# Building the S5 tables of a two-layer hybrid trunk without GpSimd, dealt out per weight unit of the first feed-forward network

## The chip, the cores and the metric

The kernel runs on one NeuronCore of a Trainium2 chip. The metric is device time in microseconds (us) of one execution. The engines are named TensorE (PE in rows), VectorE (DVE), ScalarE (ACT), GpSimd (POOL) and SyncE (SP), whose queue issues nearly all transfers; PEld in rows is TensorE's weight load.

## The reference, cut to what matters

The model is two layers on a sequence of 512 tokens of width 1024. Each layer is feed-forward network (FFN), token mixer, FFN; the first layer's mixer is an S5 state-space layer, the second's a convolution module. So there are six sub-layers: ffn0, s5, ffn2, ffn3, conv, ffn5. The first two matter here:

```python
def swiglu(h, w1, w3, w2):                # w1, w3: 1024 x 2816, w2: 2816 x 1024
    return (jax.nn.silu(h @ w1) * (h @ w3)) @ w2

# s5_mixer, for each of 64 groups of 16 channels, 64 complex states:
    mag = jnp.exp(dt * ar)
    abar_re = mag * jnp.cos(dt * ai)
    abar_im = mag * jnp.sin(dt * ai)
    f_re = (nr * ar + abar_im * ai) / den
    f_im = (abar_im * ar - nr * ai) / den
    bb_re = f_re[..., None] * br - f_im[..., None] * bi
    bb_im = f_re[..., None] * bi + f_im[..., None] * br
```

The recurrence state(t) = abar * state(t-1) + bb * u(t), read out by c, is computed in blocks of steps. For that the kernel needs tables that depend on the parameters alone: powers of abar (turns), input tables from f and b, output products of c with powers of abar, and short kernels c * abar^k * bb laid out as a Toeplitz block.

## The kernel before, in words

**Matrix products.** Every weight is loaded by SP as a unit of 128x1024 (eight blocks of 128x128; line 84) and split in two halves, a high one cast by ScalarE (L95) and a low one that is the difference (L99), by VectorE or, while `lo_engine` says so, by GpSimd. `mm3` (L111 to L113) runs three matmuls of 512 columns a block: high by high, high by low, low by high. So a unit is 24 matmuls.

**The first FFN.** The up product takes 44 units, two for each of 22 output blocks m: one unit for w1, one for w3. m = 0 and 1 belong to the entry, the loop in `ffn` takes m = 2 to 21. The block before is evacuated by five operations in a fixed order: VectorE L399, ScalarE L400 (silu), VectorE L401, ScalarE L403, VectorE L404. The down product (`proj`) takes 22 units. `want(n)` splits units ahead of their use, one or two units ahead.

**The tables.** They are made while ffn0 runs, stored to `tab_d` in device memory, and read back by the S5 layer. `s5_params` is a chain of small VectorE operations (128x32). `s5_turn` first doubles a table H on VectorE (L638 to L640), then for each of eight tiles a table E in three steps of 128x64, 128x128 and 128x256 on GpSimd (L652 to L654). `s5_ops` makes, for each of eight tiles, output products with c (L735 to L737: four powers in 128x512, a fifth in 128x128; the imaginary half on GpSimd), products with b (L749 to L751, 128x128), copies on ScalarE (L755), kernels on TensorE (L698) and their Toeplitz layout on VectorE (L710 to L716). The tables b and c come with the zero blocks of a pair of groups in them, and the products run over those too. `s5_in` makes the input tables: each tile loads one block of b (L664) and four of f (L667, from `f_d`), runs six 128x512 operations on VectorE (L674 to L680) and stores (L681).

**What sets the order.** Each engine runs its instructions in the order in which the Python program emits them. The table builders are generators in queues named D, E, Q, K, T and P. `pump(q, n)` takes n steps from queue q. How many a block m gets is written by hand in `PACE_D`, `PACE_E`, `PACE_Q0` and `PACE_Q1`; the down product takes one step of P at every eighth matmul group; what is left is flushed behind the down product.

```python
            pump("D", PACE_D[m - 2])
            pump("E", PACE_E[m - 2])
            pump("Q", PACE_Q1[m - 2])
            lo_engine[0] = POOL if bg["D"] and not bg["E"] else DVE
```

Of the kernel before, what the change touches and what calls it, by code (L numbers as in the profile page):

```python
# [7 lines left out]
F32 = mybir.dt.float32  # L8
# [3 lines left out]
P = 128  # L12
# [24 lines left out]
def trunk(ctx: ExitStack, tc: tile.TileContext, h, plan):  # L37
# [103 lines left out]
    bg = {q: [] for q in "DEKTQP"}  # L141

    def pump(q, n=1):
        while n and bg[q]:
            if next(bg[q][0], StopIteration) is StopIteration:
                bg[q].pop(0)
            else:
                n -= 1

    def flush():  # L150
        while any(bg.values()):
            for q in "DEQKTP":
                pump(q)
# [84 lines left out]
    def proj(u0, nk, rhs, post, nl, pre, xn, bias=None, lead=None, carried=None, defer=True):  # L238
# [154 lines left out]
    def ffn(e, post, pre, defer=True):  # L393
# [15 lines left out]
        for m in range(2, NF):  # L409
            ready = len(bg["K"])  # L410
            pump("Q", PACE_Q0[m - 2])
            pa, pb = psum(), psum()
            for j, ps in enumerate((pa, pb)):
                want(u0 + 2 * m + j)
                for k in range(NK):
# [3 lines left out]
                    if j == 1 and k == 3 and ready:  # L419
                        pump("K")  # L420
# [31 lines left out]
    def s5_params(tb, F):  # L452
# [6 lines left out]
        ar, ai, ldt = (prm[:, 32 * i : 32 * i + 32] for i in range(3))  # L459
        free = [s[:, j, :] for s in scr for j in range(32)]  # L460
# [4 lines left out]
        def tt(a, b, op, o=None):  # L465
            o = new() if o is None else o
# [3 lines left out]
        def ts(a, c, op, c2=None, op2=None, o=None):  # L470
            o = new() if o is None else o
# [6 lines left out]
        def stt(a, c, b, op, op2, o=None):  # L478
            o = new() if o is None else o
# [33 lines left out]
        def sincos(v, c, s):  # L513
# [97 lines left out]
        def turned():  # L611
# [3 lines left out]
            bg["T"].append(store(pst))  # L615
            yield
# [10 lines left out]
    def s5_turn(tb):  # L627

        H = page(F32).rearrange("p r (q c) -> p r q c", c=16)
        w = page(F32).rearrange("p r (q c) -> p r q c", c=16)  # L630
        DVE.memset(H[:, 0, :, 0:1], 1.0)
        DVE.memset(H[:, 1, :, 0:1], 0.0)
        for j in range(4):
            n = 1 << j
            er, ei = (v[:, j, :].unsqueeze(2).to_broadcast([P, 32, n]) for v in (tb["er"], tb["ei"]))
            re, im = H[:, 0, :, :n], H[:, 1, :, :n]
            for d, (p, q, op) in enumerate((((re, er), (im, ei), ALU.subtract), ((re, ei), (im, er), ALU.add))):
                DVE.tensor_tensor(w[:, 0, :, :n], p[0], p[1], op=ALU.mult)  # L638
                DVE.tensor_tensor(w[:, 1, :, :n], q[0], q[1], op=ALU.mult)
                DVE.tensor_tensor(H[:, d, :, n : 2 * n], w[:, 0, :, :n], w[:, 1, :, :n], op=op)  # L640
            yield
        for i in range(8):
            E = page(F32).rearrange("p r (q c) -> p r q c", q=4)
            w = page(F32).rearrange("p r (q c) -> p r q c", q=4)
            s = slice(4 * i, 4 * i + 4)
            ACT.copy(E[:, :, :, 0:16], H[:, :, s, :])  # L646
            for j in range(4, 7):
                n = 1 << j
                er, ei = (v[:, j, s].unsqueeze(2).to_broadcast([P, 4, n]) for v in (tb["er"], tb["ei"]))
                re, im = E[:, 0, :, :n], E[:, 1, :, :n]  # L650
                for d, (p, q, op) in enumerate((((re, er), (im, ei), ALU.subtract), ((re, ei), (im, er), ALU.add))):
# [6 lines left out]
    def s5_in():  # L658
# [11 lines left out]
        nxt = load(0)  # L670
        for i in range(8):
            (bt, fb), nxt = nxt, load(i + 1) if i < 7 else None
# [3 lines left out]
            DVE.tensor_tensor(fb[:, 1, :], fb[:, 0, :], bt[:, 1, :], op=M)  # L676
            yield
# [3 lines left out]
            nc.sync.dma_start(out=tab_d[i, :, 0:1024], in_=flat(fb))  # L681
            yield

    def s5_ops(tb, F):
# [742 lines left out]
```

## Time and profile before

| | |
|---|---|
| median of 3 runs | 1966.86 us (1965.58 to 1968.68) |
| the profiled execution | 1966.77 us, its span 1965.0 us |
| TensorE busy | 1878.3 us (96% of the span) |
| VectorE busy | 1144.3 us (58%) |
| ScalarE busy | 608.8 us (31%) |
| GpSimd busy | 227.0 us (12%), nearly all in the first 600 us |

TensorE is busy nearly everywhere, so the time is the sum of its matmuls, plus the places where it waits, plus the places where its clock is low. The share of busy time does not tell the last two apart: a matmul at half clock counts as busy, too. One has to look at the granted clock and at the waits, stretch by stretch.

### The profile page before, as it was taken

To read this page: it belongs to the slowest core of one execution; us is meant where nothing else is said; L and a number is where in the kernel's file an instruction comes from. 1 tells how busy PE (TensorE), PEld (TensorE's weight loads), DVE (VectorE), ACT (ScalarE), POOL (GpSimd) and SP (SyncE) were. 2 spreads that over 40 slices of the span, in tenths; PEclk is the share of its full clock that TensorE was granted. 3 is DMA by queue.
4 is the path that set the end of the run, shared out by engine and by line. 5 is a ranking of instruction groups with operands and counts; after the bars stand their busy time and mean duration, and the time that the engine had idled before them with its cause. 6 is when DMAs were issued, how large, how long until landed. Compare 5 with 4: busy or idle time off the path is not lost.

```text
span 1965.0 us, 23884 instructions
## 1 busy us (share of the span) xinstructions
PE 1878.3 (96%) x9374; PEld 1591.5 (81%) x9374; DVE 1144.3 (58%) x1796; ACT 608.8 (31%) x856; POOL 227.0 (12%) x269
## 2 busy tenths in 40 slices
PE   9978799999679999999999999999999999999997
PEld 7766588888568988888898888888888898888886
DVE  6888875758965853433267343323996785443324
ACT  5222232233214542322135222212512554232211
POOL 2437523012740000000000000000000000000000
PEclk9989899999889999999999999999999999999998
DMA  4234436945822233222223232232374023323231
GB/s 156 97 106 135 127 129 184 286 161 212 293 75 86 76 130 106 89 94 90 92 76 127 98 105 88 66 117 97 127 254 161 29 90 129 107 86 95 79 106 43
DMA packets 100129, 236.11 MB, mean 120 GB/s; under 512 B 26032, under 2 KB 41904, under 8 KB 100016
## 3 DMA queue, kind: packets, MB, share of 16 engines
q1 hardware_dynamic: 98720, 233.51, 36.2%
q8 instruction: 73, 1.20, 0.3%
q10 hardware_dynamic: 1296, 1.07, 0.2%
q14 instruction: 40, 0.33, 0.0%
HBM read 210.82 MB, written 23.72 MB: 119 GB/s over the span
## 4 chain that ended last, share of the span: by engine, by line
PE 79%; DVE 16%; issue 2%; ACT 1%; DMA 1%; POOL 1%; POOLq 0%; DVEq 0%; SPq 0%; ACTq 0%
PE ps L113 25%; PE ps L112 25%; PE ps L111 25%; PE ps L1141 2%; DVE pg L99 2%; DVE pg L467 1%; DVE pg L834 1%; PE ps L1108 1%; DVE x L341 1%; DVE tmp L337 1%; DVE pg L737 1%; DVE pg L844 1%; DVE pg L735 1%; DVE pg L736 1%; DVE tmp L401 1%
## 5 line engine op out<-in xcount | busy, mean ns | idle before, releaser
L113 PE MATMUL ps<-pg,pg 128*128 128x512 f32 (+1 forms) x2808 | 1033.6, 368 | 24.9 <-DVE pg L99 22.5
L111 PE MATMUL ps<-pg,pg 128*128 128x512 f32 (+1 forms) x2808 | 1039.3, 370 | 9.1 <-ACT pg L1275 4.7
L112 PE MATMUL ps<-pg,pg 128*128 128x512 f32 (+1 forms) x2808 | 1033.9, 368 | 4.9 <-DVE pg L173 3.4
L113 PEld LDWEIGHTS ps<-pg,pg 128*128 128x128 f32 x2808 | 533.3, 190 | 115.8 <-DVE pg L99 25.9
L111 PEld LDWEIGHTS ps<-pg,pg 128*128 128x128 f32 x2808 | 533.4, 190 | 97.6 <-ACT pg L1275 5.1
L112 PEld LDWEIGHTS ps<-pg,pg 128*128 128x128 f32 x2808 | 533.0, 190 | 97.4 <-DVE pg L173 8.2
L99 DVE TENSOR_TENSOR pg<-raw,pg 128x1024 fp32r<-128x1024 f32 x295 | 358.7, 1253 | 97.6 <-ACT pg L95 61.0
L95 ACT CAST pg<-raw 128x1024 fp32r<-128x1024 f32 x310 | 310.7, 1047 | 127.5 <-DMA raw<-w 28.2
L401 DVE TENSOR_TENSOR tmp<-ps,tmp 128x512 f32<-128x512 f32 x88 | 60.9, 692 | 247.3 <-PE ps L113 218.3
L263 DVE TENSOR_TENSOR acc<-acc,tmp 128x512 f32<-128x512 f32 (+1 forms) x54 | 33.0, 611 | 265.3 <-ACT tmp L258 265.2
L400 ACT ACTIVATE tmp<-tmp 128x512 f32<-128x512 f32 x88 | 55.6, 632 | 318.9 <-DVE tmp L399 318.9
L403 ACT CAST pg<-tmp 128x512 fp32r<-128x512 f32 x88 | 54.6, 621 | 249.9 <-DVE tmp L401 249.1
L258 ACT ACTIVATE tmp<-ps 128x512 f32<-128x512 f32 (+1 forms) x45 | 24.3, 539 | 300.8 <-PE ps L113 300.4
L404 DVE TENSOR_TENSOR pg<-tmp,pg 128x512 fp32r<-128x512 f32 x88 | 61.3, 696 | 61.1 <-ACT pg L403 61.1
L399 DVE TENSOR_TENSOR tmp<-ps,y 128x512 f32<-128x512 f32 x88 | 60.5, 688 | 27.3 <-PE ps L113 27.1
L160 ACT ACTIVATE pg<-x,gsc 128x256 fp32r<-128x256 f32 x80 | 40.8, 510 | 67.9 <-DVE x L341 67.9
L1055 DVE SCALAR_TENSOR_TENSOR pg<-pg,vec,pg 128x512 f32<-128x512 f32 x79 | 53.0, 741 | 0.0
L173 DVE SCALAR_TENSOR_TENSOR pg<-x,gsc,pg 128x256 fp32r<-128x256 f32 (+1 forms) x88 | 48.5, 553 | 2.3 <-ACT pg L201 1.8
L652 POOL TENSOR_TENSOR pg<-pg,pg 128x64 f32<-128x64 f32 (+2 forms) x48 | 27.6, 575 | 162.9 <-ACT pg L646 160.0
L341 DVE SCALAR_TENSOR_TENSOR x<-tmp,gsc,x 128x256 f32<-128x256 f32 x96 | 45.8, 478 | 0.0
L1141 PEld LDWEIGHTS ps<-pg,pg 128*128 128x128 f32 x360 | 41.0, 192 | 0.4
L1141 PE MATMUL ps<-pg,pg 128*128 128x128 f32 x360 | 41.0, 275 | 0.0
(163 smaller groups left out, 1059.2 us busy)
## 6 DMA issues: line engine op xcount, KB each, us to landing
raw<-w SPq DMA_DIRECT2D x262, 512.0 KB, 4.0
pg<-tab_d SPq DMA_DIRECT2D x24, 512.0 KB, 6.3
pg<-toep SPq DMA_DIRECT2D x20, 512.0 KB, 5.8
tab_d<-pg SPq DMA_DIRECT2D x16, 512.0 KB, 3.3
raw<-cv_w_in SPq DMA_DIRECT2D x16, 512.0 KB, 4.6
pg<-s5b SPq DMA_DIRECT2D x8, 512.0 KB, 8.8
pg<-f_d SPq DMA_DIRECT2D x32, 128.0 KB, 8.0
raw<-s_w_in SPq DMA_DIRECT2D x8, 512.0 KB, 4.2
```

Source lines behind the costliest of these rows:

```text
L95: ACT.copy(hv, r)
L99: lo_engine[0].tensor_tensor(lv, r, hv.bitcast(F32), op=ALU.subtract)
L111: PE.matmul(out, lhsT=hi[:, s, :], rhs=xh, start=start, stop=False)
L112: PE.matmul(out, lhsT=hi[:, s, :], rhs=xl, start=False, stop=False)
L113: PE.matmul(out, lhsT=lo[:, s, :], rhs=xh, start=False, stop=stop)
L341: DVE.scalar_tensor_tensor(x[:, k, cs], t[:, cs], gsc[:, post + k : post + k + 1], x[:, k, cs], op0=ALU.mult, op1=ALU.add)
L399: DVE.tensor_tensor(a, pa, e["y"], op=ALU.mult)
L400: ACT.activation(a, a, AF.Silu)
L401: DVE.tensor_tensor(a, pb, a, op=ALU.mult)
L403: ACT.copy(t[:, 0, :], a)
L404: DVE.tensor_tensor(t[:, 1, :], a, t[:, 0, :].bitcast(F32), op=ALU.subtract)
L1141: PE.matmul(ps[:, q * P : q * P + P], lhsT=op[ND * q + d], rhs=z[:, q, 8 - d : 8 - d + P], start=d == 0, stop=d == ND - 1,)
```

## The change

GpSimd no longer takes part in the tables, except that it clears buffers. The low halves of all weights, the E steps and all products go to VectorE. The products run without the zero blocks: c and b come packed (the host lays out `s5b` with 256 + 128 columns where it had 640), VectorE works on 128x320 (five powers at once) and 128x64, and ScalarE copies the results to their places between zeros. The Toeplitz layout is one VectorE addition in PSUM and four ScalarE copies. The hand-written paces are replaced by `tick(q, budget)`: each piece of work adds an estimate of its VectorE time to `cost`, and a tick hands out work until its credit is spent. In the up product there is a tick at every unit (two for each m), in the down product one at every unit. Tiles 0 and 1 of `s5_ops` stay in the up product, tiles 2 to 7 and then `s5_in` go to the down product. The loads of the parameters and of the identity move to the start of the program.

The diff, cut to its core (`...` marks what is left out):

```diff
+PREP_UP, PREP_DOWN = 2.8, 3.4
+S5_FIRST = 2
...
+    def tick(q, budget):
+        for stage in "TK":
+            now, bg[stage] = bg[stage], []
+            for g in now:
+                if next(g, StopIteration) is not StopIteration:
+                    bg[stage].append(g)
+        credit[0] += budget
+        while bg[q] and credit[0] > 0:
+            before = cost[0]
+            done = next(bg[q][0], StopIteration)
+            if done is StopIteration:
                 bg[q].pop(0)
+            elif done == "wait":
+                break
+            credit[0] -= cost[0] - before
...
-                if k % 8 == 4:
-                    pump("P")
+                if unit(m, k)[1] == 4:
+                    tick("P", PREP_DOWN)
...
-                    if j == 1 and k == 3 and ready:
-                        pump("K")
+                    if k == 3:
+                        tick("D", PREP_UP)
...
-            pump("T")
-            pump("D", PACE_D[m - 2])
-            pump("E", PACE_E[m - 2])
-            pump("Q", PACE_Q1[m - 2])
-            lo_engine[0] = POOL if bg["D"] and not bg["E"] else DVE
...
+        def double(src, w, er, ei, n):
+            re, im = src[:, 0, :, :n], src[:, 1, :, :n]
+            cost[0] += 6 * max(0.15, 0.09 + er.shape[1] * n * 0.00105)
+            for o, a, b in zip(w, (re, im, re, im), (er, ei, ei, er)):
+                DVE.tensor_tensor(o[:, :, :n], a, b, op=ALU.mult)
+            for d, op in enumerate((ALU.subtract, ALU.add)):
+                DVE.tensor_tensor(src[:, d, :, n : 2 * n], w[2 * d][:, :, :n], w[2 * d + 1][:, :, :n], op=op)
...
-                for d, (p, q, op) in enumerate((((re, er), (im, ei), ALU.subtract), ((re, ei), (im, er), ALU.add))):
-                    POOL.tensor_tensor(w[:, 0, :, :n], p[0], p[1], op=ALU.mult)
-                    POOL.tensor_tensor(w[:, 1, :, :n], q[0], q[1], op=ALU.mult)
-                    POOL.tensor_tensor(E[:, d, :, n : 2 * n], w[:, 0, :, :n], w[:, 1, :, :n], op=op)
+                double(E, w, er, ei, n)
...
         nxt = load(0)
+        yield
         for i in range(8):
-            (bt, fb), nxt = nxt, load(i + 1) if i < 7 else None
+            bt, fb = nxt
             t = page(F32)
             DVE.tensor_tensor(t[:, 0, :], fb[:, 1, :], bt[:, 1, :], op=M)
...
+            cost[0] += 2.1
+            if i < 7:
+                nxt = load(i + 1)
             yield
...
+        for v in qms + [bx, mms]:
+            POOL.memset(flat(v), 0.0)
...
+                c0, c1 = (v[:, j].unsqueeze(2).to_broadcast([P, 4, 5, 16]) for j in (0, 1))
+                w0, w1 = (pows[n].unsqueeze(3).to_broadcast([P, 4, 5, 16]) for n in (n0, n1))
+                DVE.tensor_tensor(qc[:, r], c0, w0, op=M)
+                DVE.tensor_tensor(t5, c1, w1, op=M)
+                DVE.tensor_tensor(qc[:, r], qc[:, r], t5, op=A)
+                cost[0] += 1.25
...
+            for s, f in groups:
+                ACT.copy(
+                    bx[s].rearrange("p r (q k g) -> p (r q) k g", q=4, k=4)[:, :, :, f],
+                    bb[s].rearrange(rq).unsqueeze(2).to_broadcast([64, 8, 4, 16]),
+                )
...
-            tb["turn"] = lambda: bg["E"].append(s5_turn(tb))
+            tb["turn"] = lambda: None
             yield from s5_params(tb, F)
-            bg["Q"].append(s5_ops(tb, F))
+            bg["D"].append(s5_turn(tb))
+            bg["D"].append(s5_ops(tb, F, range(S5_FIRST)))
+            bg["P"].append(s5_ops(tb, F, range(S5_FIRST, 8)))
             bg["P"].append(s5_in())
```

Three places show what this does to the order on the engines. In the rows, pg, raw and tmp are buffers (pg a page of working memory, raw a weight as loaded), ps is PSUM, acc an accumulator, and x3 means three like it.

**VectorE, from the evacuation of block 1 on.** Before (the low half of unit 7 and those of units 8 to 16 stand on GpSimd and are not among these rows):

```order
L399 TENSOR_TENSOR tmp_394<-ps_125,y_344 128x512
L401 TENSOR_TENSOR tmp_394<-ps_126,tmp_394 128x512
L404 TENSOR_TENSOR pg_398<-tmp_394,pg_398 128x512
L475 TENSOR_SCALAR pg_404<-tmp_406 128x32
L473 TENSOR_SCALAR pg_404<-pg_404 128x32 x3
L480 SCALAR_TENSOR_TENSOR pg_404<-pg_404 128x32 x2
L473 TENSOR_SCALAR pg_404<-pg_404 128x32
```

After the change, the rows that follow the evacuation of block 1 (L417 is the old L404, L475 to L490 the small operations of `s5_params`, L98 the old L99):

```order
L482 TENSOR_SCALAR pg_117<-pg_117 128x32
L484 TENSOR_SCALAR pg_117<-pg_117 128x32
L518 CAST pg_117<-pg_117 128x32
L475 TENSOR_TENSOR pg_117<-pg_117 128x32
L475 TENSOR_TENSOR pg_117<-pg_117,tmp_119 128x32
L482 TENSOR_SCALAR pg_117<-pg_117 128x32 x3
L490 SCALAR_TENSOR_TENSOR pg_117<-pg_117 128x32 x3
L475 TENSOR_TENSOR pg_117<-pg_117 128x32
L484 TENSOR_SCALAR pg_117<-pg_117 128x32 x2
L475 TENSOR_TENSOR pg_117<-pg_117 128x32 x2
L490 SCALAR_TENSOR_TENSOR pg_117<-pg_117 128x32 x2
L98 TENSOR_TENSOR pg_487<-raw_319,pg_486 128x1024
```

The low half of unit 7 (`pg_487`) now stands on VectorE, behind 18 small operations and the two evacuations. Fifteen more small operations stand ahead of the first of these evacuations, where there were none.

**The E steps in the up product.** Before, GpSimd, behind its last low halves:

```order
L99 TENSOR_TENSOR pg_787<-raw_622,pg_786 128x1024
L99 TENSOR_TENSOR pg_793<-raw_709,pg_792 128x1024
L652 TENSOR_TENSOR pg_1049<-pg_1048,pg_402 128x4x16
L653 TENSOR_TENSOR pg_1049<-pg_1048,pg_402 128x4x16
L654 TENSOR_TENSOR pg_1048<-pg_1049 128x4x16
```

After the change, VectorE over one block m and the start of the next tile (L645 and L647 are the multiplications and additions of `double`):

```order
L98 TENSOR_TENSOR pg_1247<-raw_1069,pg_1246 128x1024
L98 TENSOR_TENSOR pg_1253<-raw_1153,pg_1252 128x1024
L412 TENSOR_TENSOR tmp_1258<-ps_1078,y_370 128x512
L414 TENSOR_TENSOR tmp_1258<-ps_1079,tmp_1258 128x512
L417 TENSOR_TENSOR pg_1262<-tmp_1258,pg_1262 128x512
L645 TENSOR_TENSOR pg_921<-pg_1195,pg_115 128x4x32 x4
L647 TENSOR_TENSOR pg_1195<-pg_921 128x4x32 x2
L645 TENSOR_TENSOR pg_921<-pg_1195,pg_115 128x256 x4
L647 TENSOR_TENSOR pg_1195<-pg_921 128x4x64 x2
```

GpSimd has 82 rows in all after the change, where it had 274. The steps have moved from GpSimd into the gaps between the low halves and evacuations on VectorE.

**The input tables in the down product, VectorE.** Before:

```order
L674 TENSOR_TENSOR pg_2540<-pg_2527,pg_2526 128x512
L675 TENSOR_TENSOR pg_2540<-pg_2527,pg_2526 128x512
L676 TENSOR_TENSOR pg_2527<-pg_2527,pg_2526 128x512
L99 TENSOR_TENSOR pg_2554<-raw_2386,pg_2553 128x1024
L678 TENSOR_TENSOR pg_2527<-pg_2527,pg_2526 128x512
L679 TENSOR_TENSOR pg_2527<-pg_2527,pg_2540 128x512
L680 TENSOR_TENSOR pg_2527<-pg_2527,pg_2540 128x512
L99 TENSOR_TENSOR pg_2588<-raw_2461,pg_2587 128x1024
```

After the change (L695 to L704 are the old L674 to L680, L754 is the addition of the Toeplitz layout):

```order
L98 TENSOR_TENSOR pg_2704<-raw_2505,pg_2703 128x1024
L754 TENSOR_TENSOR ps_2681<-ps_2681,pg_2245 128x4x32
L695 TENSOR_TENSOR pg_2730<-pg_2635,pg_2634 128x512
L696 TENSOR_TENSOR pg_2730<-pg_2635,pg_2634 128x512
L697 TENSOR_TENSOR pg_2635<-pg_2635,pg_2634 128x512
L702 TENSOR_TENSOR pg_2635<-pg_2635,pg_2634 128x512
L703 TENSOR_TENSOR pg_2635<-pg_2635,pg_2730 128x512
L704 TENSOR_TENSOR pg_2635<-pg_2635,pg_2730 128x512
```

A whole tile now stands between two low halves at places, where before half a tile did.

## Rows read from the trace of the kernel before

**Rows 1.** TensorE's waits, 36 to 470 us: releaser, total, times, longest.

```profile
PE ps L113 <- DVE pg L99: 22.1, 7, 7.3
PE ps L614 <- DVE pg L608: 5.5, 1, 5.5
PE ps L111 <- ACT pg L95: 2.6, 2, 2.3
```

**Rows 2.** Windows: PE, PEld, DVE, ACT, POOL busy; clock, DMA share, GB/s.

```profile
100.00:150.00 50.00, 39.08 (x163) 31.03 (x162) 43.89 (x140) 13.70 (x19) 22.26 (x32) 0.90 0.34 106
150.00:200.00 50.00, 42.20 (x188) 33.65 (x187) 42.80 (x67) 11.68 (x19) 33.58 (x53) 0.90 0.44 133
200.00:250.00 50.00, 37.19 (x157) 29.41 (x156) 45.15 (x75) 12.34 (x17) 25.50 (x31) 0.83 0.44 130
```

**Rows 3.** TensorE's timeline, sums at both ends of two FFNs (start, us).

```profile
36.23 1.02 PE L118 MATMUL ps<-acc,ones 128*128 128x512 f32 x2
...
430.54 0.59 PE L118 MATMUL ps<-acc,ones 128*128 128x256 f32 x2
...
679.72 1.02 PE L118 MATMUL ps<-acc,ones 128*128 128x512 f32 x2
...
1009.25 0.59 PE L118 MATMUL ps<-acc,ones 128*128 128x256 f32 x2
```

**Rows 4.** TensorE's timeline: after a wait, and around a tile's table products.

```profile
175.21 0.80 PE L113 MATMUL ps<-pg,pg 128*128 128x512 f32 x1 [4.78 <-DVE pg L99]
...
176.23 0.63 PE L112 MATMUL ps<-pg,pg 128*128 128x512 f32 x1
176.66 0.63 PE L113 MATMUL ps<-pg,pg 128*128 128x512 f32 x1
...
252.30 0.39 PE L112 MATMUL ps<-pg,pg 128*128 128x512 f32 x1
...
253.89 0.39 PE L113 MATMUL ps<-pg,pg 128*128 128x512 f32 x1
...
255.82 0.48 PE L111 MATMUL ps<-pg,pg 128*128 128x512 f32 x1
```

**Rows 5.** The timeline of GpSimd, then VectorE, from 47.5 to 59 us.

```profile
47.88 9.48 POOL L99 TENSOR_TENSOR pg<-raw,pg 128x1024 fp32r<-128x1024 f32 x4 [26.74 <-ACT pg L95]
...
47.70 4.98 DVE L473 TENSOR_SCALAR pg<-pg 128x32 f32<-128x32 f32 x3
...
57.65 1.32 DVE L480 SCALAR_TENSOR_TENSOR pg<-pg 128x32 f32<-128x32 f32 x6
```

**Rows 6.** VectorE's timeline: evacuations from 40 us, tables and halves from 117 us.

```profile
40.75 0.68 DVE L399 TENSOR_TENSOR tmp<-ps,y 128x512 f32<-128x512 f32 x1
...
44.12 0.68 DVE L399 TENSOR_TENSOR tmp<-ps,y 128x512 f32<-128x512 f32 x1
...
117.01 0.28 DVE L638 TENSOR_TENSOR pg<-pg,pg 128x128 f32<-128x128 f32 x1
...
118.71 0.42 DVE L638 TENSOR_TENSOR pg<-pg,pg 128x256 f32<-128x256 f32 x1
...
121.10 2.35 DVE L99 TENSOR_TENSOR pg<-raw,pg 128x1024 fp32r<-128x1024 f32 x2
```

**Rows 7.** Busy time by window, while the down product builds the input tables.

```profile
350.00:360.00 10.00, 10.00 (x46) 8.28 (x45) 7.67 (x12) 2.11 (x2) 0.00 (x0) 1.00 1.03 278
```

**Rows 8.** Line 674: what VectorE sat idle for before it, us and times.

```profile
  DMA pg<-f_d: 17.8, 6
```

**Rows 9.** The page, DMA issues: count, KB each, median us to landing.

```profile
raw<-w SPq DMA_DIRECT2D x262, 512.0 KB, 4.0
...
tab_d<-pg SPq DMA_DIRECT2D x16, 512.0 KB, 3.3
...
pg<-s5b SPq DMA_DIRECT2D x8, 512.0 KB, 8.8
pg<-f_d SPq DMA_DIRECT2D x32, 128.0 KB, 8.0
```

More of the change, by code (lines that the diff above doesn't have):

```diff
@@ L139, in y_tile @@
         return statp.tile([P, T], F32, tag="y", name=nm("y"))
[L141 to L145, printed above, removed]
-                bg[q].pop(0)
-            else:
-                n -= 1
+    bg = {q: [] for q in "DPKT"}
+    cost, credit = [0.0], [0.0]
+    def tick(q, budget):
[9 more added lines that the diff above has]
+            if done is StopIteration:
+                bg[q].pop(0)
+            elif done == "wait":
+                break
+            credit[0] -= cost[0] - before
+        if not bg[q]:
+            credit[0] = 0.0
     def flush():
         while any(bg.values()):
-            for q in "DEQKTP":
-                pump(q)
+            for q in "DP":
+                tick(q, 100.0)
     FULL = slice(0, T)
@@ L465, in tt @@
         def tt(a, b, op, o=None):
+            cost[0] += 0.18
             o = new() if o is None else o
@@ L470, in ts @@
         def ts(a, c, op, c2=None, op2=None, o=None):
+            cost[0] += 0.18
             o = new() if o is None else o
@@ L478, in stt @@
         def stt(a, c, b, op, op2, o=None):
+            cost[0] += 0.18
             o = new() if o is None else o
@@ L627, in s5_turn @@
     def s5_turn(tb):
-        H = page(F32).rearrange("p r (q c) -> p r q c", c=16)
-        w = page(F32).rearrange("p r (q c) -> p r q c", c=16)
+        def double(src, w, er, ei, n):
[5 more added lines that the diff above has]
+                DVE.tensor_tensor(src[:, d, :, n : 2 * n], w[2 * d][:, :, :n], w[2 * d + 1][:, :, :n], op=op)
+        H, wp = page(F32).rearrange("p r (q c) -> p r q c", c=16), flat(page(F32))
+        w = [wp[:, 256 * a : 256 * a + 256].rearrange("p (q c) -> p q c", c=8) for a in range(4)]
         DVE.memset(H[:, 0, :, 0:1], 1.0)
@@ L681, in s5_in, with s5_ops @@
             nc.sync.dma_start(out=tab_d[i, :, 0:1024], in_=flat(fb))
+            cost[0] += 2.1
             yield
-    def s5_ops(tb, F):
+    def s5_ops(tb, F, tiles):
         M, A, S = ALU.mult, ALU.add, ALU.subtract
@@ L713, in toeplitz @@
                 s = slice(32 * t, 32 * t + 32)
-                DVE.tensor_copy(mv[s, :, t:4, :], pv[s, :, 0 : 4 - t, :])
-                DVE.tensor_tensor(mv[s, :, t, :], mv[s, :, t, :], v[s, 4], op=A)
+                ACT.copy(mv[s, :, t:4, :], pv[s, :, 0 : 4 - t, :])
             nc.sync.dma_start(out=tab_d[i, :, 3072:3584], in_=mm)
             yield
-        nxt = load(0)
+        nxt = load(tiles[0])
         yield
-        for i in range(8):
-            v, nxt = nxt, load(i + 1) if i < 7 else None
-            qm, wk = page(F32).rearrange("p r (q k g) -> p r q k g", q=4, k=4), flat(page(F32))
-            w, w2 = wk[:, :T], tmp()
-            q4 = wk[:, T : T + 256].rearrange("p (r q g) -> p r q g", r=2, q=4)
-            bb = wk[:, T + 256 :].rearrange("p (r q g) -> p r q g", r=2, q=4)
+        for i in tiles:
+            v, d = nxt
+            if i != tiles[-1]:
+                nxt = load(i + 1)
+            qm = qms[i % 2].rearrange("p r (q k g) -> p r q k g", q=4, k=4)
+            q4 = q4s[i % 2]
@@ new lines, in s5_ops @@
+            f0, f1 = (Fv[:, 3, i, r].unsqueeze(2).to_broadcast([P, 4, 16]) for r in range(2))
+            for r, (x0, op) in enumerate(((2, S), (3, A))):
+                DVE.tensor_tensor(bb[:, r], f0, v[:, x0], op=M)
+                DVE.tensor_tensor(t1, f1, v[:, 5 - x0], op=M)
+                DVE.tensor_tensor(bb[:, r], bb[:, r], t1, op=op)
+            cost[0] += 0.85
+            rq = "p r q f -> p (r q) f"
+            for s, f in groups:
+                ACT.copy(
+                    qm[s, :, :, :, f].rearrange("p r q k f -> p (r q) k f"),
+                    qc[s, :, :, 0:4].rearrange("p r q k f -> p (r q) k f"),
+                )
+                ACT.copy(q4[s, :, :, f].rearrange(rq), qc[s, :, :, 4].rearrange(rq))
@@ L745, in s5_ops @@
                 nc.sync.dma_start(out=dst[:, r, :, 3], in_=q4[:, r])
[L746 to L756 removed]
+            yield
+            while busy:
+                yield "wait"
+            busy.append(i)
+            for s, f in groups:
+                ACT.copy(
+                    bx[s].rearrange("p r (q k g) -> p (r q) k g", q=4, k=4)[:, :, :, f],
+                    bb[s].rearrange(rq).unsqueeze(2).to_broadcast([64, 8, 4, 16]),
+                )
+            bg["K"].append(kernels(i, d, qm))
             yield
```

102 lines of the change are left out of this document (49 added, 53 removed).

## The prediction

> **What bounds the kernel now.** I read the page first: TensorE is busy in 96% of the span, so time can come only from its waits, its clock and its own work. Then the timeline at the sums that open and close an FFN. From the opening sum of ffn0 to the first sum of its down product 394.31 us pass, in ffn2, which has the same products and no tables, 329.53 us [rows 3]. The reader is to see the difference, 64.8 us: that is all that the tables cost TensorE. A part of it is work. Seven matmul intervals, from 252.30 to 253.89 us, give 0.227 us each, and the 1.93 us from 253.89 to 255.82 us hold one matmul and a tile's table products, so these cost 1.70 us [rows 4], and eight tiles 13.6 us. This stays. What can be won is 64.8 - 13.6 = 51 us.
>
> The list of waits says where: TensorE waits 22.1 us for low halves from VectorE, in 7 waits, 5.5 us for the f tables (L608) and 2.6 us for high halves from ScalarE [rows 1], together 30 us. The windows say where the rest is. From 100 to 250 us TensorE is busy for only 37 to 42 us in 50, and its granted clock is 0.90, 0.90 and 0.83 [rows 2]. There are two levels, 1.2 and 2.4 GHz, so a mean of 0.90 is half clock in 20% of a window, and the three make 10 + 10 + 17 = 37 us at half clock, which cost about half of that, 18.5 us. The timeline shows it: behind a wait of 4.78 us the matmuls start 0.43 us apart [rows 4]. 30 + 18.5 is nearly the 51 us. Eight waits go with it, so a long wait costs some 2.3 us of clock besides itself.
>
> Why is VectorE late? It is busy for 44 us in 50 there [rows 2], but partly with little work. While GpSimd runs four low halves from 47.88 us on, 2.37 us each, three VectorE operations of 128x32 take 4.98 us; with GpSimd idle, six take 1.32 us, 0.22 each [rows 5]. GpSimd is slow, VectorE waits beside it, the low halves queue behind that, and TensorE behind these.
>
> **The change part by part.**
>
> *GpSimd out of the tables.* All the waits of rows 1 belong to this pattern: **-51 us** if nothing takes their place. Its buffer clearing is not in the trace. GpSimd needs 2.37 us for two inputs of 128x1024 [rows 5], so I bound one at 0 to 2.4 us. It is hidden as GpSimd does nothing else then; uncovered it would hold ScalarE's copies once, for up to 2.4 us.
>
> *Unit 7.* Its low half stood first on GpSimd and was done at 50.25 us. TensorE wants it at 36.23 + 0.86 (the sum) + 59 x 0.227 = 50.5 us [rows 3, 4], just in time. Now VectorE takes it. The first evacuation could start at 40.75 us [rows 6]; 15 small operations stand ahead of it (3.3 us at 0.22), two evacuations take 2 x 3.37 us (40.75 to 44.12 us), 18 small operations 4.0 us, the half 1.2 us (two in 2.35) [rows 5, 6]: ready at 56.0 us, 5.5 us late. Operations that don't wait for each other run closer, so 3 to 5.5 us; I take **+5 us**.
>
> *Up product, VectorE's sum.* A block m now holds an evacuation of 3.4 us, two low halves of 2.35 us and two ticks of 2.8 us by the kernel's own costs. How true are these? Six operations of 128x128 take 1.70 us (117.01 to 118.71), six of 128x256 2.39 us (to 121.10) [rows 6], and the step of 128x64 I estimate at 1.3 us, six small ones: an E tile is 5.4 us where the code counts 4.44. So 5.6 us of credit are 6.7 us, and a block takes 12.5 us of VectorE where TensorE needs 48 x 0.227 = 10.9 us. Over some nine blocks of E steps and the first two tiles VectorE falls back by 14 us. Against that it may be ahead: the next low half is due 120 matmuls (27.2 us) after the matmuls that the evacuation needs, and between them lie 12.5 us of work, so its lead is at most 14.7 us. The two are equal, so the wait is between 0 and 14 us; I take **+2 us**, as the chain of small operations leaves most of the lead.
>
> *First table product.* It stands one unit (5.4 us) behind the operations that feed it, on a VectorE that has used up its lead, and six ScalarE copies. The nearest row is the f tables' wait of 5.5 us [rows 1]; 0 to 8 us, I take **+3 us**. Placing by ScalarE itself I cost at nothing: ScalarE is busy for 11 to 14 us in 50 [rows 2].
>
> *Input tables in the down product.* Eight tiles are now handed out over 240 matmuls, 54.4 us or 6.8 us a tile. A tile moves 512 KB of b, 4 x 128 KB of f and a store of 512 KB, 1.57 MB, beside a weight of 512 KB every 5.44 us (96 GB/s) [rows 9]. At a DMA share of 1.03 the queues moved 278 GB/s [rows 7]. That leaves 182 GB/s, 8.6 us a tile, so the loads end 14 us late over eight tiles, and VectorE waits for them with the low halves of the down weights queued behind it. Loads that land after 8.0 to 8.8 us [rows 9] already made it wait 17.8 us in six waits [rows 8]. Low halves stand up to 48 matmuls (10.9 us) ahead of their use, which covers the first wait and a part of the rest. Bounds are 0 and 20 us; I take **+8 us**.
>
> The Trainium skill, page "SBUF — State Buffer", section "SBUF: two separate sides", gives about 358 GB/s between device memory and a core. By it a tile would need 1.57 MB at 262 GB/s, an estimate of 6.0 us, the loads would keep up and this term would be 0. The 278 GB/s of the row speak against that, and the row decides for me.
>
> *Clock.* Unit 7, the first table product and two of the input tiles are long waits: 4 x 2.3 = **+9 us**.
>
> *Moved loads.* The two parameter loads now stand near the front of SP's queue; the waits they could cause would be of VectorE's first small operations, at a place where nobody waits for these: 0. The tables' own transfers stand behind the same weight loads as before.
>
> Sum: -51 + 5 + 2 + 3 + 8 + 9 = -24 us. The profiled execution took 1966.77 us, which is the median of the runs (1966.86), so **1943 us**.
>
> **The rivals.**
>
> *Everything but unit 7 is covered.* VectorE keeps its lead and the transfers keep up. 1966.8 - 51 + 5 + 2.3 = 1923 us. For it: the intervals of the new waits but unit 7 begin at 0. Against it: the sums for VectorE and for the transfers are both over what TensorE leaves them.
>
> *The transfers keep up, the rest as forecast.* The term of 8 us and two waits' clock go: 1943 - 12.6 = 1930 us. For it: b and f were loaded beside other things before, too. The page's figure (above) would lead here.
>
> *Same.* New waits give back all that the old ones cost. That needs 51 us where I count 27; or GpSimd was not what slowed VectorE. Rows 5 speak against the second, and the order has 82 GpSimd rows where there were 274, so the change does what it says. 1963 to 1971 us.
>
> *Slower: the input tables' transfers hold the down product.* If the queues move less than 260 GB/s, the point from which this decides, a tile takes 1.57 MB at 164 GB/s or 9.6 us and more, 2.8 us over its 6.8. VectorE stops the low halves at each of eight tiles: 22.4 us, and 3 us for the first load, which is now used at once, in place of 8 us, +17. Each of eight waits takes 2.3 us of clock, 18 in place of 4.6, +14. 1943 + 31 = 1974 us. For it: VectorE already waits at this place, for loads that had more time. Against it: 278 GB/s in the row, and TensorE that waits also asks for fewer weights.
>
> **How the numbers follow.** Forecast 0.50 (1930 to 1958 us), all covered 0.20, transfers keep up 0.12, same 0.08, slower 0.10. 0.2% is 3.9 us, about what a measurement of this kernel can tell from no change. Faster by more: 0.50 + 0.20 + 0.12 = 0.82. The range leaves out the slow rival, half of "same" and the fast end of "all covered": 1922 to 1965 us. The likeliest case stands at 1943 us.
>
> **What would show it.** Right: VectorE's 128x32 operations near 0.2 us throughout; TensorE's clock at 1.00 in most of 100 to 250 us; one wait of about 5 us near 50 us, for a low half; a wait at the first table product of tile 0; in the down product waits of VectorE for `f_d` and TensorE behind them. Wrong: more than 30 us of new waits, or none in the down product; a clock below 0.9 anywhere in the up product; a change of the time outside ffn0, where nothing but the flush is touched.

## The result, and the profile after

The changed kernel takes 1931.45 us (median of 4 runs, 1930.56 to 1933.42), beside 1967.77 us for the kernel before (median of 4 runs). The ratio is 0.9818, 95% interval 0.9801 to 0.9835. It is 36 us faster; the forecast was 24 us (1943), with a range from 1922 to 1965 us.

Nearly all of it comes from ffn0. The timeline of the changed kernel at the sums that open its first FFN and its down product's first statistics (start us, us):

```profile
35.24 1.02 PE L117 MATMUL ps<-acc,ones 128*128 128x512 f32 x2
...
394.24 0.59 PE L117 MATMUL ps<-acc,ones 128*128 128x256 f32 x2
```

359.0 us, where there were 394.3 [rows 3]: 35.3 us less, of the 36.6 us by which the spans of the two profiled executions differ (1965.0 and 1928.4 us). Another 1.0 us lies ahead of the opening sum. The tables' own 13.6 us and the 329.5 us of an FFN without tables would be 343.1 us, so 15.9 us of excess are left, of 51.2 us (64.8 less the table products). TensorE's waits in the changed kernel, 36 to 470 us (releaser, total us, times, longest):

```profile
PE ps L112 <- DVE pg L98: 9.5, 4, 3.4
PE ps L919 <- DVE pg L909: 5.8, 1, 5.8
PE ps L110 <- ACT pg L94: 0.8, 1, 0.8
```

This list answers to rows 1: 22.1 us for low halves (L98 is the old L99) have become 9.5, and the f tables' wait of 5.5 us is gone. L919 belongs to the S5 layer, behind ffn0. Where the five waits of L112 and L110 lie, the timeline of TensorE shows (wait and releaser in brackets):

```profile
50.05 0.50 PE L110 MATMUL ps<-pg,pg 128*128 128x512 f32 x1 [0.83 <-ACT pg L94]
...
54.14 0.50 PE L112 MATMUL ps<-pg,pg 128*128 128x512 f32 x1 [3.35 <-DVE pg L98]
...
332.58 0.50 PE L112 MATMUL ps<-pg,pg 128*128 128x512 f32 x1 [0.76 <-DVE pg L98]
...
345.83 0.50 PE L112 MATMUL ps<-pg,pg 128*128 128x512 f32 x1 [2.08 <-DVE pg L98]
...
365.72 0.80 PE L112 MATMUL ps<-pg,pg 128*128 128x512 f32 x1 [3.27 <-DVE pg L98]
```

Two belong to unit 7, near 50 us, three to the input tables in the down product. Between 55 and 332 us there is none. The windows of the changed kernel (PE, PEld, DVE, ACT, POOL busy; then clock, DMA share, GB/s) show the other half of the gain:

```profile
50.00:100.00 50.00, 46.59 (x197) 38.12 (x198) 43.05 (x195) 15.66 (x20) 0.00 (x0) 0.97 0.32 106
100.00:150.00 50.00, 50.00 (x224) 41.35 (x223) 42.42 (x122) 17.27 (x27) 0.00 (x0) 1.00 0.46 150
150.00:200.00 50.00, 50.00 (x230) 41.74 (x229) 36.95 (x100) 18.55 (x32) 4.27 (x6) 1.00 0.52 156
200.00:250.00 50.00, 50.00 (x230) 41.70 (x230) 22.39 (x27) 18.92 (x26) 0.00 (x0) 1.00 0.36 116
```

From 100 to 250 us TensorE is busy throughout at full clock, where it was busy for 37 to 42 us in 50 at 0.83 to 0.90 [rows 2].

### The profile page after: what moved, and what is told of

Its sections match the earlier page's. It is cut to its first block, busy times and chain, and to the rows that moved or that the text cites. A ratio compares the mean times of both kernels' runs of the same rounds, so it can differ in the third digit from the quotient of the medians.

```text
span 1928.4 us, 23797 instructions
## 1 busy us (share of the span) xinstructions
PE 1867.4 (97%) x9374; PEld 1587.3 (82%) x9374; DVE 1100.8 (57%) x1886; ACT 636.9 (33%) x920; POOL 89.2 (5%) x79
## 4 chain that ended last, share of the span: by engine, by line
PE 86%; DVE 9%; DMA 2%; issue 1%; ACT 1%; SPq 1%; POOLq 0%; POOL 0%; DVEq 0%; ACTq 0%
PE ps L112 27%; PE ps L111 27%; PE ps L110 27%; PE ps L1199 2%; DMA pg<-f_d 1%; DVE pg L98 1%; DVE pg L892 1%; PE ps L1166 1%; DVE x L354 1%; DVE tmp L350 1%; PE ps L740 1%; DVE pg L902 1%; PE ps L117 0%; DVE pg L186 0%; DVE pg L903 0%
## 5 line engine op out<-in xcount | busy, mean ns | idle before, releaser
L110 PE MATMUL ps<-pg,pg 128*128 128x512 f32 (+1 forms) x2808 | 1036.8, 369 | 7.4 <-ACT pg L1333 4.7
L112 PE MATMUL ps<-pg,pg 128*128 128x512 f32 (+1 forms) x2808 | 1029.8, 367 | 9.9 <-DVE pg L98 9.8
L112 PEld LDWEIGHTS ps<-pg,pg 128*128 128x128 f32 x2808 | 531.5, 189 | 97.9 <-DVE pg L98 11.9
L110 PEld LDWEIGHTS ps<-pg,pg 128*128 128x128 f32 x2808 | 532.3, 190 | 95.5 <-ACT pg L1333 5.1
L98 DVE TENSOR_TENSOR pg<-raw,pg 128x1024 fp32r<-128x1024 f32 x305 | 368.3, 1244 | 109.9 <-ACT pg L94 63.5
L417 DVE TENSOR_TENSOR pg<-tmp,pg 128x512 fp32r<-128x512 f32 x88 | 61.0, 693 | 61.8 <-ACT pg L416 61.8
L173 ACT ACTIVATE pg<-x,gsc 128x256 fp32r<-128x256 f32 x80 | 40.8, 510 | 67.8 <-DVE x L354 67.8
L350 DVE TENSOR_TENSOR tmp<-pg,y 128x256 f32<-128x256 f32 x96 | 39.6, 418 | 0.4
```

The source lines that it names most:

```text
L98: lo_engine[0].tensor_tensor(lv, r, hv.bitcast(F32), op=ALU.subtract)
L110: PE.matmul(out, lhsT=hi[:, s, :], rhs=xh, start=start, stop=False)
L112: PE.matmul(out, lhsT=lo[:, s, :], rhs=xh, start=False, stop=stop)
L350: DVE.tensor_tensor(t[:, cs], hs[k][:, cs], y[:, cs], op=ALU.mult)
L417: DVE.tensor_tensor(t[:, 1, :], a, t[:, 0, :].bitcast(F32), op=ALU.subtract)
```

## The experiments

Each was timed against the kernel before in rounds of its own; a ratio is to the kernel before, with its 95% interval. In the rounds of the experiments the kernel before had medians of 1967.62, 1968.05 and 1968.38 us. "ffn0" is the stretch between the two sums above, in the profiled execution, which is not always the median one: with the E steps on GpSimd it is the fastest of four (1937.39 us), with two ticks less the slowest (1930.93 us).

| kernel | median us | ratio | ffn0, us |
|---|---|---|---|
| before | 1967.77 | 1 | 394.3 |
| changed | 1931.45 | 0.9818 (0.9801 to 0.9835) | 359.0 |
| before, no GpSimd in the tables | 1972.38 | 1.0027 (1.0017 to 1.0038) | 399.6 |
| changed, 10 low halves on GpSimd | 1942.01 | 0.9866 (0.9846 to 0.9887) | 372.4 |
| changed, E steps on GpSimd | 1941.78 | 0.9872 (0.9848 to 0.9896) | 367.0 |
| changed, ticks by two | 1931.67 | 0.9816 (0.9801 to 0.9831) | 362.4 |
| changed, ticks by four | 1941.73 | 0.9865 (0.9848 to 0.9883) | 371.4 |
| changed, 3.6 of credit | 1948.69 | 0.9904 (0.9887 to 0.9920) | 376.6 |
| changed, products twice | 1951.49 | 0.9919 (0.9904 to 0.9934) | 379.8 |
| changed, f loaded once | 1922.26 | 0.9772 (0.9756 to 0.9788) | 351.5 |
| changed, two ticks less | 1927.45 | 0.9797 (0.9782 to 0.9811) | 353.6 |
| changed, slower input tables | 1926.41 | 0.9787 (0.9772 to 0.9802) | 353.5 |
| both of these | 1920.59 | 0.9758 (0.9744 to 0.9773) | 347.2 |
| both, price 3.0 | 1917.88 | 0.9749 (0.9734 to 0.9763) | 344.8 |

**GpSimd taken out of the kernel before, and nothing else.**

```diff
-                    POOL.tensor_tensor(w[:, 0, :, :n], p[0], p[1], op=ALU.mult)
+                    DVE.tensor_tensor(w[:, 0, :, :n], p[0], p[1], op=ALU.mult)
...
-                    eng = (DVE, POOL)[r]
+                    eng = DVE
...
-            lo_engine[0] = POOL if bg["D"] and not bg["E"] else DVE
+            lo_engine[0] = DVE
```

> The kernel before with VectorE in place of GpSimd for the E steps, the imaginary half of the products and the low halves; paces, zero blocks and places unchanged. Theory (the time came from GpSimd slowing VectorE): most of the 51 us of waits and low clock goes, VectorE's small operations take 0.2 us, 1932 to 1952 us. Rival (the time came from dealing the work out evenly, and from less work): VectorE has some 90 us more to do in bursts that the hand-written paces set, TensorE waits for low halves as much as before, 1960 us or more.

It is slower than before, by 0.27%. The theory here was that of the prediction, and it fell. VectorE's small operations are indeed fast now, the groups of VectorE from 36 to 300 us say (busy us, mean ns; the mean was 309 ns in the kernel before):

```profile
L467 DVE TENSOR_TENSOR pg<-pg 128x32 f32<-128x32 f32 x97 | 13.4, 193 | 0.8
```

But TensorE waits as it did; its waits from 30 to 440 us, and two windows, of this kernel:

```profile
PE ps L113 <- DVE pg L99: 21.7, 6, 7.7
PE ps L111 <- ACT pg L95: 10.0, 3, 4.4
PE ps L698 <- ACT pg L755: 3.8, 2, 3.5
```

```profile
100.00:150.00 50.00, 46.50 (x201) 38.44 (x200) 44.36 (x146) 11.09 (x16) 0.00 (x0) 0.93 0.38 117
...
200.00:250.00 50.00, 33.62 (x142) 26.46 (x141) 42.75 (x107) 9.81 (x14) 0.00 (x0) 0.80 0.40 115
```

VectorE is busy for 1161.4 us in all, where it was busy for 1144.3, although it now does all that GpSimd did for the tables: what it took over is only 17 us longer than the blocking that went. The hand-written paces hand it out in lumps; one of them lasts 12.2 us, from 136.10 to 148.29 us, between an evacuation and the next two low halves. That the lumps make the low halves late here is my reading; the ticks by four below test it in the changed kernel. To take GpSimd out brings nothing by itself, but to put it back into the changed kernel costs some 10 of the 36 us, as the next two kernels show.

**Low halves of units 7 to 16 back on GpSimd, in the changed kernel.**

```diff
-                lo_engine[0].tensor_tensor(lv, r, hv.bitcast(F32), op=ALU.subtract)
+                (POOL if 7 <= u <= 16 else lo_engine[0]).tensor_tensor(lv, r, hv.bitcast(F32), op=ALU.subtract)
```

> The changed kernel with the low halves of units 7 to 16 back on GpSimd, 10 of 2.37 us. Theory: VectorE is blocked for about 24 us between 48 and 105 us and saves 12 us of its own, so 12 us net fall on its lead; the wait of 4 us at unit 7 goes, waits of 3 to 12 us come in the up product, 1931 to 1942 us. Rival (GpSimd beside VectorE is harmless when the work is dealt out evenly): only the wait at unit 7 goes, 1925 to 1927 us.

10.6 us slower than the changed kernel, at the far end of the theory. The wait at unit 7 did not go, it shrank to 0.81 and 1.71 us. The timeline of GpSimd and VectorE in this kernel shows the cause again, and TensorE's timeline the effect:

```profile
51.52 9.38 POOL L98 TENSOR_TENSOR pg<-raw,pg 128x1024 fp32r<-128x1024 f32 x4 [30.05 <-ACT pg L94]
...
51.56 2.35 DVE L518 CAST pg<-pg 128x32 int32<-128x32 f32 x1
53.95 2.30 DVE L475 TENSOR_TENSOR pg<-pg 128x32 f32<-128x32 f32 x1
...
61.41 0.64 DVE L490 SCALAR_TENSOR_TENSOR pg<-pg 128x32 f32<-128x32 f32 x3
```

```profile
124.41 0.50 PE L112 MATMUL ps<-pg,pg 128*128 128x512 f32 x1 [1.53 <-DVE pg L98]
...
192.78 0.50 PE L112 MATMUL ps<-pg,pg 128*128 128x512 f32 x1 [2.80 <-DVE pg L98]
...
199.78 0.55 PE L740 MATMUL ps<-pg,pg 128*128 128x128 f32 x1 [3.51 <-ACT pg L806]
```

Four halves take 9.38 us on GpSimd, and a cast or an addition of 128x32 beside them takes 2.3 us, three operations behind them 0.64 together. The Trainium skill, page "SBUF — State Buffer", section "SBUF: two separate sides", describes a pair of ports that GpSimd and VectorE share as an exclusive lock, held for a whole instruction; that one operation of VectorE lasts as long as one of GpSimd (2.35 and 2.30 us against a fourth of 9.38, 2.35 us) agrees. The reader is to see the distance: VectorE is blocked at times between 51 and 98 us (ten halves), and TensorE waits at 124, 193 and 200 us. In between VectorE carries the delay along. The pair of low halves that it starts at 111.31 us in the changed kernel starts at 123.14 us here, and the one of 163.91 us at 175.81, so 11.8 and 11.9 us later (the opening sum comes 1.5 us later). What is lost is VectorE's lead, and TensorE waits where the rest of it does not suffice.

**E steps back on GpSimd, in the changed kernel**: `double` gets an engine, and the calls for E pass POOL.

> The changed kernel with the E steps of all eight tiles back on GpSimd, the ticks unchanged. Theory: VectorE sheds 43 us but stands still beside about 80 us of GpSimd, its low halves come late again, with half clock behind the longer waits: 1945 to 1965 us. Rival (less work on VectorE is what counts): 1926 to 1932 us.

10.3 us slower than the changed kernel, less than expected (1945 at least), but no gain, so the rival falls. TensorE's waits of this kernel:

```profile
PE ps L112 <- DVE pg L98: 10.1, 4, 3.7
PE ps L740 <- ACT pg L806: 4.4, 1, 4.4
```

L740 is the first table product. The timelines of VectorE and ScalarE ahead of it show two things:

```profile
167.78 5.04 DVE L417 TENSOR_TENSOR pg<-tmp,pg 128x512 fp32r<-128x512 f32 x1 [0.69 <-ACT pg L416]
...
182.23 0.62 ACT L416 CAST pg<-tmp 128x512 fp32r<-128x512 f32 x1 [5.67 <-POOL pg L647]
```

An operation of VectorE that lasts 0.69 us in other blocks lasts 5.04 us beside GpSimd. And an evacuation on ScalarE waits 5.67 us for GpSimd's last E step, whose result it does not use; I read this as a wait for a page of working memory. GpSimd takes 9.5 us for an E tile here (162.75 to 172.24 us), where VectorE takes 4.04. So this kernel shows the blocking and GpSimd's slowness together; the blocking by itself is shown by the kernel with the low halves on GpSimd.

**The same work in lumps.**

```diff
-                    if k == 3:
-                        tick("D", PREP_UP)
+                    if k == 3 and (2 * m + j) % 4 == 0:
+                        tick("D", 4 * PREP_UP)
```

> The changed kernel with one tick of twice the credit at every second unit of the up product. Theory (VectorE may fall back by a lead of up to 14.7 us before TensorE waits, so small bursts are free): 5.6 of credit, some 6.7 us at once, is covered, 1930 to 1936 us. Rival (the even dealing itself is what counts, any burst delays low halves): 1940 us or more.

> The changed kernel with one tick of four times the credit at every fourth unit of the up product; no GpSimd, the same work, only handed out in lumps of some 13.4 us. Theory (without GpSimd it is lumps over VectorE's lead that cost the waits of the kernel before without GpSimd): an evacuation, two low halves and a lump are 19 us of the 27.2 us between an evacuation and the next low half's use, the rest of the lead is gone by the E steps: new waits of 5 to 20 us, 1937 to 1960 us. Rival (the work that was saved is what counts, not its order): 1930 to 1935 us.

By two: no difference in the median (1931.67). In its profiled execution ffn0 is 3.4 us longer; 1.0 us of this is waits (11.3 us, where there were 10.3), and the clock is lower from 50 to 100 us (0.93, where it was 0.97). By four: 1941.73, 10.3 us slower with nothing else changed. Lumps of one block (up to 6 us in the trace) are covered, lumps of two (10.1 us from 150.05 to 160.14 us) are not. Two waits of the kernel with lumps by four that the changed kernel doesn't have:

```profile
189.23 0.50 PE L110 MATMUL ps<-pg,pg 128*128 128x512 f32 x1 [2.98 <-ACT pg L94]
...
281.05 1.20 PE L740 MATMUL ps<-pg,pg 128*128 128x128 f32 x4 [4.69 <-ACT pg L806]
```

**More credit a tick.** `PREP_UP` is 3.6 in place of 2.8.

> The changed kernel with 3.6 in place of 2.8 us of credit at a tick of the up product. Theory (VectorE falls back by its sum against 10.9 us a block): a block then holds 14.3 us, VectorE falls back 3.4 us a block over some seven blocks, 24 us against a lead of at most 14.7; TensorE waits about 9 us more, with clock, 1938 to 1946 us. Rival (the lead is larger than I count, or the operations are cheaper): no new wait, 1930 to 1933 us.

1948.69 us, a little over the expected range. From 100 to 150 us TensorE is busy for 50.00 us in 50; the waits come where VectorE's lead is used up (timeline of TensorE):

```profile
162.11 0.79 PE L112 MATMUL ps<-pg,pg 128*128 128x512 f32 x1 [6.10 <-DVE pg L98]
...
169.11 3.55 PE L740 MATMUL ps<-pg,pg 128*128 128x128 f32 x16 [2.69 <-ACT pg L806]
```

**VectorE's products of the output tables twice.** The loops over the halves of `qc` and `bb` run twice, at an unchanged price.

> The changed kernel with every VectorE product of the output tables made twice, 12 operations or some 4 us more a tile, at an unchanged price, so that VectorE has about the work that the zero blocks would give it. Theory (in the down product VectorE has 7.1 us a tile and uses 6.3): it falls back by 3 us a tile over six tiles, 19 us against a cover of 10.9 us, with new waits for low halves of some 8 us and clock, 1937 to 1948 us. Rival (VectorE has room, the smaller products save nothing that counts): 1930 to 1934 us.

1951.49 us, 20 us slower than the changed kernel and over the expected range. The work saved does count: VectorE has no room for it in the down product. From 270 to 320 us it is busy for 48.45 us in 50, where in the changed kernel it is busy for 32.99 us from 265 to 315 us. TensorE's waits of this kernel:

```profile
PE ps L112 <- DVE pg L98: 10.2, 4, 3.4
PE ps L740 <- ACT pg L806: 9.2, 5, 2.5
```

The theory's 8 us of new waits for low halves did not come: the first row was 9.5 us in the changed kernel. The part that I had not expected is the second row: 9.2 us in five waits at the table products themselves, one unit behind operations that are now late. This kernel stands in for the zero blocks; it doesn't run them, and it adds more work than they did. VectorE's products take 67.8 us here against 34.0 in the changed kernel, 33.8 us more; with the zero blocks, in the kernel before without GpSimd, they take 60.3 us, 26.3 more.

**f loaded once**, for tile 0, and used for all tiles: `for t in range(4 if i == 0 else 0)` in the load, with a page of its own for the result.

> The changed kernel in which the input tables load f for tile 0 alone and use it for all eight tiles, so that seven times 512 KB of loads are left out (the tables of tiles 1 to 7 are then not those of the model). Theory (the rate of the queues holds the down product): a tile moves 1.05 MB, 5.8 us at 182 GB/s, under its 6.8 us; the waits for low halves of 0.76, 2.08 and 3.27 us in the down product go, with 1.7 us of clock, 1923 to 1925 us. Rival (each transfer's latency holds it, with b still landing after 8 us): VectorE still waits several us a tile, TensorE's waits stay, 1929 to 1932 us.

1922.26 us, 9.2 us less, a little more than expected; no wait is left in the down product. So it is the loads of f that hold it. That it is their amount, and not their latency, is a reading, as both go with them. For it: b is still loaded for every tile and lands in 5.2 us (median), where it took 7.2 in the changed kernel.

**Two ticks less at the start**, for unit 7.

```diff
-                    if k == 3:
+                    if k == 3 and (u0 or (m, j) not in ((2, 1), (3, 0))):
```

> The changed kernel without the second and third tick of the first FFN's up product (15 and 18 small operations go behind the low half of unit 7). Theory: the low half is done at about 49 us, before TensorE wants it, and the two waits of 0.83 and 3.35 us with 1.6 us of clock go: 1925 to 1927 us. Rival: VectorE is short of time in the whole up product, so the wait moves on to a later unit: 1929 to 1932 us.

1927.45 us, 4.0 us less, a little short of the 1925 to 1927 us expected. The two waits near 50 us are gone, and the clock from 50 to 100 us is 1.00. A wait of 0.5 us appears at the first table product, so most of the work put off is covered, but not all. The intervals of this kernel and of the changed one overlap a little, so the profile carries this reading, not the time alone: ffn0 is 5.4 us shorter. (The profiled execution as a whole is no faster than the changed kernel's, as its opening sum comes only at 39.59 us, 4.35 us later; in the other runs here it comes between 35.2 and 36.9.)

**Slower input tables.** The price of a half tile is 3.4 in place of 2.1, the first load has one, too: one half tile a unit.

> The changed kernel with a price of 3.4 in place of 2.1 us on each half tile of the input tables, and on the first load, so that a unit of the down product gets one half tile: 10.9 us a tile in place of 6.8. Theory (the queues need 8.6 us a tile): the three waits of the down product go, 6.1 us, with 1.7 us of clock: 1923 to 1925 us. Rival: the last tile falls behind the down product and its store is late for the S5 layer, or the wait for f stays as it is latency: 1929 us or more.

1926.41 us, 5.0 us less, where 6 to 8 were expected: the three waits are gone, but a part of the rival came true. The last tile falls into the flush, and TensorE waits 2.1 us for the accumulator behind it. This interval, too, touches that of the changed kernel (0.9802 against 0.9801).

**Both, and both with price 3.0.**

> The changed kernel with both edits, the two ticks less and the slower input tables. Theory: the gains add, 5.8 + 7.8 us, 1917 to 1920 us, and TensorE has no wait over 1 us in ffn0. Rival: work put off in the up product comes out in the down product, gains do not add, 1923 us or more.

> The changed kernel with two ticks less and a price of 3.0 in place of 3.4 on a half of the input tables, so that the last tile comes before the end of the down product. Theory: the wait of 2.1 us at the end of ffn0 goes, nothing else moves, 1917.5 to 1919.5 us. Rival: tiles come too fast for the queues again, 1921 us or more.

1920.59 us is 10.9 us less than the changed kernel, so the single gains of 4.0 and 5.0 us add up, a little short of the theory by the 2.1 us that TensorE still waits at the end of ffn0. With the last tile ahead of the flush that goes, too: 1917.88 us. This is the fastest of all, 0.9749 (0.9734 to 0.9763), clear of the changed kernel's interval. Its list of waits of TensorE, 30 to 440 us, ends the account:

```profile
PE ps L111 <- DVE pg L186: 0.5, 2, 0.2
PE ps L741 <- ACT pg L807: 0.3, 1, 0.3
```

ffn0 takes 344.8 us there, 1.7 us over the 343.1 that the table products leave.

## Why the prediction was right, and where it was not

The direction and the range held, and the place: nearly everything lies in ffn0. Step by step:

- **What could be won, 51 us.** Right: the fastest kernel above, with two edits more, has 49.5 us of it (394.3 - 344.8).
- **"GpSimd out of the tables: -51 us if nothing takes their place."** This step failed as an account of the cause. The waits of rows 1 do not belong to GpSimd alone: without it, and with the old lumps and the old amount of work, they are as long. What holds them off is several things together, as each alone, undone in the changed kernel, gives back 10 to 20 us: no GpSimd beside VectorE (10.6, and 10.3 with GpSimd's slowness in it), no lumps over one block (10.3), fewer VectorE operations in the products (20, by a doubling that is more than the zero blocks were). These prices do not add up to the gain; my reading is that they draw on one reserve, VectorE's lead over TensorE, but no run undid two of them at once. That the sum still came near is in part luck: "if nothing takes their place" hung on the even dealing and the smaller work, which no run had priced then; taking GpSimd out would not have made it true by itself.
- **Unit 7, 5 us.** Right, and a little less: 0.83 + 3.35 us. VectorE's timeline in the changed kernel follows the steps of the sum:

```profile
42.96 0.68 DVE L412 TENSOR_TENSOR tmp<-ps,y 128x512 f32<-128x512 f32 x1
...
46.33 0.68 DVE L412 TENSOR_TENSOR tmp<-ps,y 128x512 f32<-128x512 f32 x1
...
49.70 0.17 DVE L482 TENSOR_SCALAR pg<-pg 128x32 f32<-128x32 f32 x1
...
52.87 1.22 DVE L98 TENSOR_TENSOR pg<-raw,pg 128x1024 fp32r<-128x1024 f32 x1
```

  The evacuations start at 42.96 us, 3.37 us apart, and the 18 small operations take 3.17 us (I had 4.0).
- **Up product, 2 us, and first table product, 3 us.** Both 0. The mis-sized term is the E tile, 5.4 us by rows 6. It takes 4.04 us (VectorE's timeline, two successive tiles):

```profile
126.74 0.62 DVE L645 TENSOR_TENSOR pg<-pg,pg 128x64 f32<-128x64 f32 x4
127.28 0.35 DVE L647 TENSOR_TENSOR pg<-pg 128x64 f32<-128x64 f32 x2
127.56 0.89 DVE L645 TENSOR_TENSOR pg<-pg,pg 128x128 f32<-128x128 f32 x4
...
128.77 1.42 DVE L645 TENSOR_TENSOR pg<-pg,pg 128x256 f32<-128x256 f32 x4
...
130.78 0.62 DVE L645 TENSOR_TENSOR pg<-pg,pg 128x64 f32<-128x64 f32 x4
```

  Six operations of 128x128 take 1.21 us (127.56 to 128.77) and six of 128x256 2.01 us, where rows 6 have 1.70 and 2.39 us. `double` puts four multiplications first that don't wait for each other; the rows that I took had two and then one that waits for them. That it is the order, and not the table, the kernel before without GpSimd shows, which runs the E steps on VectorE in the old order (VectorE's timeline):

```profile
123.49 0.29 DVE L652 TENSOR_TENSOR pg<-pg,pg 128x128 f32<-128x128 f32 x1
...
125.08 0.68 DVE L735 TENSOR_TENSOR pg<-pg,pg 128x512 f32<-128x512 f32 x1
```

  Its six operations of 128x128 take 1.59 us; with 1.30 us for 128x64 and 2.38 for 128x256 a tile is 5.3 us there, nearly what I had. For the new order the code's own price, 4.44, was the better one. So 5.6 us of credit are 5.1 us, and a block holds 3.4 + 2.35 + 5.1 = 10.9 us, TensorE's own pace: by this sum VectorE does not fall back, and TensorE has no wait from 55 to 332 us. With 3.6 of credit it has.
- **Input tables, 8 us.** 0.76 + 2.08 + 3.27 = 6.1 us, by the mechanism given. VectorE's timeline at the first operation of six of the eight tiles:

```profile
309.81 0.69 DVE L695 TENSOR_TENSOR pg<-pg,pg 128x512 f32<-128x512 f32 x1 [11.80 <-DMA pg<-f_d]
...
317.62 0.68 DVE L695 TENSOR_TENSOR pg<-pg,pg 128x512 f32<-128x512 f32 x1
...
327.32 0.69 DVE L695 TENSOR_TENSOR pg<-pg,pg 128x512 f32<-128x512 f32 x1 [3.30 <-DMA pg<-f_d]
...
342.55 0.69 DVE L695 TENSOR_TENSOR pg<-pg,pg 128x512 f32<-128x512 f32 x1 [2.93 <-DMA pg<-f_d]
...
359.26 0.69 DVE L695 TENSOR_TENSOR pg<-pg,pg 128x512 f32<-128x512 f32 x1 [4.10 <-DMA pg<-f_d]
...
365.75 0.69 DVE L695 TENSOR_TENSOR pg<-pg,pg 128x512 f32<-128x512 f32 x1
```

  The first load is waited for 11.8 us, and TensorE doesn't notice: the low halves stand that far ahead. VectorE's next three waits for f, 3.30, 2.93 and 4.10 us, are followed by TensorE's three, 0.76, 2.08 and 3.27 us. The seven tiles from 317.62 to 365.75 us come 8.0 us apart, between the 6.8 at which they are handed out and my 8.6. By the Trainium skill, page "SBUF — State Buffer", section "SBUF: two separate sides" (358 GB/s), this term would have been 0; the waits were there, so the measurement decides.
- **Clock, 9 us.** Some 3.3. Of five waits only the 3.35 and the 3.27 us were followed by half clock. Windows of 5 us in the changed kernel:

```profile
55.00:60.00 5.00, 5.00 (x17) 3.92 (x16) 4.79 (x13) 1.05 (x1) 0.00 (x0) 0.68 0.56 160
325.00:330.00 5.00, 5.00 (x24) 4.14 (x23) 2.61 (x4) 1.05 (x1) 0.00 (x0) 1.00 1.02 376
345.00:350.00 5.00, 4.17 (x18) 3.47 (x19) 4.96 (x8) 0.20 (x1) 0.00 (x0) 1.00 0.62 185
365.00:370.00 5.00, 4.28 (x12) 3.44 (x13) 4.85 (x7) 0.25 (x1) 0.00 (x0) 0.66 0.44 153
```

  A clock of 0.68 and of 0.66 is 3.2 and 3.4 us at half speed, half of which is lost; behind the wait of 2.08 us (345 us) it stayed at 1.00. I had taken a mean over waits of up to 7.3 us. One trace does not fix this price, though. In the kernel with f loaded once the same wait of 3.35 us at unit 7 is followed by 6.8 us at half clock (0.93, 0.50 and 0.89 in the three windows from 50 to 65 us), and so it is with slower input tables and with the products twice; with the E steps on GpSimd it is 3.4 us again. A wait of this length cost 1.7 or 3.4 us of clock.

New waits and clock sum to 10.3 + 3.3 = 13.6 us where I had 27; the rest of the excess of 15.9 us I can't name. So the forecast erred on the side of caution, by terms whose intervals began at 0. The slow rival's mechanism is there, at a sixth of its price. The rival in which the transfers keep up, 1930 us, is nearest in time for the wrong reason: the transfers did not keep up.

Open: how the gain splits between packed products and their placing by ScalarE, as no kernel ran the zero blocks with even dealing; and the share of the work that moved to the down product, which was not varied. Nor did any kernel undo the new Toeplitz layout, which spares VectorE as much as the packing does: L710 to L715 take 28.6 us in the kernel before without GpSimd, the one addition in their place (L754) takes 2.3 us.

## What to carry to other kernels

When an engine that waits beside another is the cause of late work, count what it will have to do once the other's work is its own; the one can be as long as the other. Look for the reserve, the lead of the engine that prepares over the one that consumes, in us, and hand out work so that no lump is larger than it: here lumps of up to 6 us were free and lumps of 10 us cost 10 us. For transfers, hand out at the rate at which the queues move them, not at the rate at which the engine could use them.

## What was not expected of the hardware

Six operations of 128x128 on the same table took 1.59 us in one order and 1.21 us in another: VectorE starts operations that don't wait for each other before the one ahead has ended (four of 128x64 and the next start within 0.54 us, 0.135 us each, where one of them lasts 0.22). And the DMA queues moved 376 GB/s from 325 to 330 us, with the share at 1.02, against 278 GB/s at 1.03 before [rows 7], so the share alone did not tell what the queues could move. The loads of f read one row into 32 partitions; whether this is why, no run shows.
